# The first MLP matrix: the rounded half of each weight tile by a casting transfer from DRAM instead of a copy on ScalarE

## The chip, the cores and the metric

The kernel runs on one core of a Trainium2 chip. The metric is the device time of one execution in microseconds (us). The kernel before takes 880.09 us, the median of three runs between 879.93 and 880.3 us. The engines are named as in the profile: PE (TensorE, the matrix unit; PEld is its weight load), DVE (VectorE), ACT (ScalarE), POOL (GpSimd) and SP (SyncE, which here only issues transfers). Each engine works through its own list of instructions in order; an instruction that waits holds up what stands behind it on that engine.

## The reference

The kernel computes one decoder layer on 512 tokens of width 1024 in float32: a normalised input goes to a gated linear recurrence and to sliding-window attention, both are merged and projected, then comes an MLP, a gated embedding and a last normalisation. The change touches the MLP alone:

```python
u = rmsnorm(x, norm_mlp_g[i]) @ w_up[i]                      # 512 x 1024 by 1024 x 4096
x = x + jnp.square(jax.nn.relu(u)) @ w_down[i]               # 512 x 4096 by 4096 x 1024
```

## The kernel before

**Two halves of every number.** PE multiplies operands of type fp32r, a float32 rounded to fewer bits. To keep float32 accuracy, each operand is held as two tiles: a rounded high part and the rest. A weight tile `wr` (128 x 1024 float32, 512 KB, loaded by an SP transfer) is split in two steps: ACT copies it with a cast into `wh` (fp32r), then DVE subtracts, `wl = wr - wh`. A product is then three matmuls: high by high, high by low, low by high. `split` (lines 134 to 141) does both steps, `load_w` (line 155) loads and splits a tile.

**Buffers.** `wr`, `wh` and `wl` have four buffers each (`WRB`, `WB`), shared in turn by all the weights of the kernel. The ACT copy of a tile can begin only when PE has finished with the tile that was four places ahead in the same buffer.

**The MLP.** `up_w(f)` (line 992) fetches tile f of the 32 tiles of `w_up`. The work goes in four quarters q. In each, `up` (line 1107) multiplies eight up tiles, 24 matmuls of 512 columns each; ACT takes the result through relu (`rt`) and square (`F`), DVE forms sums of blocks in `F`, and both are split into `uf`. Then `down` (line 1137) uses seven block products in place of eight: 14 weight tiles, 12 matmuls each, formed from eight loaded tiles (`wd`, six buffers, and two `wr` buffers). The results are added by DVE into `xk`, the running sum of the layer (line 1157).

**The entry into the MLP.** `out_proj` (line 997), the projection before the MLP, ends with four block products summed in PSUM tiles X, Y and Z and added by DVE into `xk` (line 1023). The MLP's input `x1` is `xk` transposed on PE (`two_columns_of`, line 983: two of the eight blocks of 128 channels at a time), then split by ACT and DVE (lines 140 and 141). Blocks 0 to 3 are transposed before the last product of `out_proj`, blocks 4 to 7 after its last sum into `xk` rows 256 to 511. `begin_up` (line 1056) interleaves the first two up tiles with this: the first four blocks of tile 0, the transposes of blocks 4 to 7, then the first half of tile 1 and the second halves of both.

**What sets the order.** The program's text gives the dependences; a scheduler that weighs estimated costs lays out each engine's list, so an edit in one place may change the order of other instructions nearby. Transfers issued by SP and by POOL stand in two separate queues, each in order. POOL issues few transfers: around the MLP six that add `q1` into `xk` (line 1033) and, in the last quarter, six that add a scaled product (line 1167).

Of the kernel before, what the change touches and what calls it, by code (L numbers as in the profile page):

```python
# [11 lines left out]
F32R = mybir.dt.float32r  # L12
# [4 lines left out]
P = 128  # L17
# [3 lines left out]
KT = D // P  # L21
# [8 lines left out]
WB = 4  # L30
# [6 lines left out]
def block_kernel(  # L37
# [29 lines left out]
    nc = tc.nc  # L67
    V, A, G, T = nc.vector, nc.scalar, nc.gpsimd, nc.tensor


    def pool(stack, name, **kw):
        return stack.enter_context(tc.tile_pool(name=name, bufs=1, reuse_waits="tile", **kw))
# [4 lines left out]
    wp = pool(ctx, "wp")  # L77
# [9 lines left out]
    def nm(s):  # L87
        n_names[0] += 1
        return f"{s}_{n_names[0]}"
# [30 lines left out]
    def tk(n):  # L120
        return tp_.tile([P, NH * (DV + 1)], F32, tag="tk", bufs=4, name=nm(n))
# [7 lines left out]
    def r32(t):  # L129
        return t.bitcast(F32)  # L130

    last_low = [None]

    def split(dst, src, scale=None):

        if scale is None:
            A.copy(dst[0], src)  # L137
            last_low[0] = V.tensor_sub(dst[1], src, r32(dst[0]))  # L138
        else:
            A.activation(dst[0], src, AF.Copy, scale=scale)  # L140
            V.scalar_tensor_tensor(dst[1], src, scale, r32(dst[0]), ALU.mult, ALU.subtract)
# [8 lines left out]
    def load_raw(src, n):  # L150
        raw = wp.tile([P, 1024], F32, tag="wr", bufs=WRB, name=nm("wr"))
        nc.sync.dma_start(out=raw[:, :n], in_=src)
        return raw

    def load_w(src, n, dims, raw=None):

        if raw is None:
            raw = load_raw(src, n)
        parts = [wp.tile([P, 1024], F32R, tag=t, bufs=WB, name=nm(t))[:, :n] for t in ("wh", "wl")]
        split(parts, raw[:, :n])  # L160
        return [q.rearrange("p (k c) -> p k c", k=dims) for q in parts]
# [178 lines left out]
    for m in range(NT):  # L340
# [10 lines left out]
        t = sp.tile([P, 256], F32, tag="vs", bufs=4, name=nm("vs"))  # L351
# [127 lines left out]
    for m in range(NT):  # L479
        t = tk("vm").rearrange("p (h d) -> p h d", h=NH)  # L480
# [87 lines left out]
    with tc.issue_after(last_mm[0].ins):  # L568
        for t in range(NT):
            for s in range(t + 1):  # L570
                c = (t * NT + s) * 4
                T.transpose(pgc[:, c : c + 4], gg[t][:, s * P : (s + 1) * P], ident[:4, :4])
            c = (NT * NT + t) * 4
# [416 lines left out]
            split(dst[k + c], ps[:, c, :], g[:, k + c : k + c + 1])  # L990

    def up_w(f):
        return load_w(w_up[f], KT * P, KT)

    _, x1 = big_hl("x1")

# [59 lines left out]
    def begin_up():  # L1056

        ps, w = [ps_g(), ps_g()], [up_w(0), up_w(1)]

        def part(f, k):  # L1060
            mm_T(ps[f], [q[:, k : k + 4, :] for q in w[f]], x1[k : k + 4], k == 0, k == 4)

        part(0, 0)
        two_columns_of(x1, 4, gmlp)
        two_columns_of(x1, 6, gmlp)
        part(1, 0)
        part(0, 4)
        part(1, 4)
        return ps
# [37 lines left out]
    def up(q, uf):  # L1107
        fs = None
        for f in range(8):
            if q == 0 and f < 2:  # L1110
                ps = begun[f]
            else:
                ps = ps_g()
                mm_T(ps, up_w(q * 8 + f), x1)
            a = mp.tile([P, 512], F32, tag="rt", bufs=3, name=nm("rt"))
            A.activation(a, ps, AF.Relu)
            if f % 2 == 0:
                fs = F()
            o = 2 * (f % 2)
            done = A.activation(fs[:, o : o + 2, :].rearrange("p a b -> p (a b)"), a, AF.Square)  # L1120
            if q == 0 and f == 2:
                with tc.issue_after(done.ins):
                    squares()
            if f % 2:
                hl = [np_.tile([P, 7 * 256], F32R, tag="uf", bufs=8, name=nm("uf")) for _ in range(2)]

                cut = 3 * 256 if f == 7 else 0
                if cut:
                    split([t[:, :cut] for t in hl], fs[:, 1:4, :].rearrange("p a b -> p (a b)"))
                V.tensor_add(fs[:, S1, :], fs[:, A21, :], fs[:, A22, :])  # L1130
                V.tensor_sub(fs[:, S3, :], fs[:, A11, :], fs[:, A21, :])
                V.tensor_sub(fs[:, S2, :], fs[:, S1, :], fs[:, A11, :])
                V.tensor_sub(fs[:, S4, :], fs[:, A12, :], fs[:, S2, :])  # L1133
                split([t[:, cut:] for t in hl], fs[:, 1 + cut // 256 :, :].rearrange("p a b -> p (a b)"))
                uf.append(hl)
# [302 lines left out]
```

## Time and profile before

| What | Value |
|---|---|
| Time, median of three runs | 880.09 us |
| The profiled execution, its own time | 879.82 us |
| Its span, first to last instruction | 878.0 us |
| PE busy | 866.8 us of the span |
| DVE busy | 657.2 us |
| ACT busy | 483.5 us |
| POOL busy | 34.1 us |
| Granted PE clock, mean | 0.998 |

The profile page gives the busy time of each engine, the span in forty slices, the chain of waits that ended last, and the costliest groups of instructions. A timeline row reads: start, duration, engine, line, operation, output tile `<-` input tiles, shape, count, and in brackets the idle time of that engine before it with what ended it. The landing time of a transfer counts from its issue to its last byte's signal. A line number can be that of a helper: all weight splits stand under lines 137 (ACT) and 138 (DVE).

### The profile page before, as it was taken

Reading aid. Unit: us, or ns where it says so; the run is one execution under the profiler, and the core shown is the slowest. Engines: PE = TensorE matmul, PEld = TensorE weight load, DVE = VectorE, ACT = ScalarE, POOL = GpSimd, SP = SyncE. Lnnn points to the kernel's source line nnn. Section 1 sums busy time; section 2 is a strip of 40 time slices with the busy share of each in tenths; the row PEclk is TensorE's granted clock in tenths of the full one; section 3 lists DMA queues with packets and bytes.
Section 4 is the critical chain, followed back from the end, with each engine's and each line's share of the span. In section 5 each row is a group of like instructions: output and inputs, shape, how many; then the busy total and the mean of one; then the engine's idle time right before and its main releaser. Section 6 shows DMA issues by size and latency. Waiting matters only on the chain.

```text
span 878.0 us, 11545 instructions
## 1 busy us (share of the span) xinstructions
PE 866.8 (99%) x4372; PEld 725.6 (83%) x4372; DVE 657.2 (75%) x966; ACT 483.5 (55%) x803; POOL 34.1 (4%) x58
## 2 busy tenths in 40 slices
PE   8999999999999999999999999999999999999996
PEld 7888889998777777788888888888888888888886
DVE  6999887875789876665896669756956794698557
ACT  6684554544676768743344665356435634564843
POOL 1111010000000000000020000000000000020000
PEclk9999999999999999999999999999999999999999
DMA  7765244435122162274244612530352054125302
GB/s 266 211 180 186 73 150 169 165 111 196 52 73 72 49 199 88 97 240 144 72 75 145 236 49 71 197 106 10 124 185 75 1 186 149 49 52 141 121 0 96
DMA packets 32793, 106.74 MB, mean 122 GB/s; under 512 B 4573, under 2 KB 4573, under 8 KB 32738
## 3 DMA queue, kind: packets, MB, share of 16 engines
q1 hardware_dynamic: 27570, 93.15, 31.2%
q0 software_dynamic: 5024, 12.59, 5.9%
q8 instruction: 34, 0.56, 0.3%
q10 hardware_dynamic: 144, 0.26, 0.1%
q14 instruction: 21, 0.17, 0.1%
HBM read 91.30 MB, written 8.40 MB: 114 GB/s over the span
## 4 chain that ended last, share of the span: by engine, by line
PE 90%; DVE 4%; ACT 3%; DMA 2%; issue 1%; SPq 0%; ACTq 0%; DVEq 0%
PE psg L171 50%; PE psp L171 23%; PE psa L171 7%; PE pst L171 4%; PE psa L831 1%; PE pst L747 1%; DVE wl L138 1%; DMA wr<-in_w_vsif 1%; ACT lm L712 1%; PE psa L819 1%; PE psa L689 1%; PE psa L690 1%; ACT wh L137 0%; DMA wr<-in_w_gb 0%; PE psp L980 0%
## 5 line engine op out<-in xcount | busy, mean ns | idle before, releaser
L137 ACT CAST wh<-wr 128x1024 fp32r<-128x1024 f32 x138 | 144.8, 1051 | 180.3 <-PE psg L171 74.8
L138 DVE TENSOR_TENSOR wl<-wr,wh 128x1024 fp32r<-128x1024 f32 x138 | 167.8, 1219 | 85.9 <-ACT wh L137 84.6
L171 PE MATMUL psg<-x,wh 128*128 128x512 f32 x512 | 157.7, 389 | 0.0
L171 PE MATMUL psp<-wh,uf 128*128 128x512 f32 x448 | 138.6, 389 | 0.0
L171 PEld LDWEIGHTS psg<-x,wh 128*128 128x128 f32 x512 | 96.0, 188 | 19.9
L171 PE MATMUL psg<-x,wl 128*128 128x512 f32 x256 | 99.6, 389 | 0.0
L171 PEld LDWEIGHTS psp<-wh,uf 128*128 128x128 f32 x448 | 84.1, 188 | 17.5
L171 PE MATMUL psp<-wl,uf 128*128 128x512 f32 x224 | 87.2, 389 | 0.0
L171 PE MATMUL psg<-h,wh 128*128 128x512 f32 x256 | 81.1, 395 | 0.7 <-DVE rc L715 0.7
L137 ACT CAST wh<-wd 128x1024 fp32r<-128x1024 f32 x44 | 46.2, 1052 | 54.0 <-PE psp L171 21.9
L138 DVE TENSOR_TENSOR wl<-wd,wh 128x1024 fp32r<-128x1024 f32 x44 | 53.1, 1217 | 14.7 <-ACT wh L137 14.5
L171 PEld LDWEIGHTS psg<-x,wl 128*128 128x128 f32 x256 | 48.0, 188 | 10.0
L171 PEld LDWEIGHTS psg<-h,wh 128*128 128x128 f32 x256 | 47.0, 188 | 11.2 <-issue 1.6
L171 PE MATMUL psg<-h,wl 128*128 128x512 f32 x128 | 50.5, 395 | 0.0
L138 DVE TENSOR_TENSOR uf<-F,uf 128x1792 fp32r<-128x1792 f32 (+2 forms) x20 | 33.0, 1652 | 21.8 <-ACT uf L137 21.8
L171 PEld LDWEIGHTS psp<-wl,uf 128*128 128x128 f32 x224 | 42.0, 188 | 8.7
L171 PE MATMUL psg<-yb,wh 128*128 128x512 f32 x128 | 41.3, 402 | 0.1
L171 PE MATMUL psg<-ya,wh 128*128 128x512 f32 x128 | 39.5, 390 | 0.0
L137 ACT CAST uf<-F 128x1792 fp32r<-128x1792 f32 (+2 forms) x20 | 27.9, 1396 | 20.5 <-DVE F L1133 20.4
L1157 DVE SCALAR_TENSOR_TENSOR xk<-psp,r,xk 128x512 f32<-128x512 f32 x48 | 33.7, 744 | 5.5 <-PE psp L171 5.2
L171 PE MATMUL psg<-hS,wh 128*128 128x256 f32 x192 | 35.6, 284 | 0.0
L171 PE MATMUL psa<-h,wh 128*128 128x256 f32 x192 | 35.3, 285 | 0.2 <-ACT p L625 0.2
(322 smaller groups left out, 1745.6 us busy)
## 6 DMA issues: line engine op xcount, KB each, us to landing
wr<-in_w_up SPq DMA_DIRECT2D x32, 512.0 KB, 3.3
wd<-in_w_down SPq DMA_DIRECT2D x24, 512.0 KB, 3.7
wr<-in_w_qsw SPq DMA_DIRECT2D x8, 512.0 KB, 4.3
gd<-gr POOLq DMA_DIRECT2D x8, 512.0 KB, 3.7
wr<-in_w_qkml SPq DMA_DIRECT2D x8, 512.0 KB, 3.2
wr<-in_w_b SPq DMA_DIRECT2D x8, 512.0 KB, 3.2
gl<-gd SPq DMA_DIRECT2D x8, 512.0 KB, 3.4
wr<-in_w_a SPq DMA_DIRECT2D x8, 512.0 KB, 4.4
```

Of the source, the lines that this page charges most:

```text
L137: A.copy(dst[0], src)
L138: last_low[0] = V.tensor_sub(dst[1], src, r32(dst[0]))
L171: last_mm[0] = T.matmul(ps, l, r, start=first and i == 0, stop=last and i == len(ops) - 1, skip_group_check=parts)
L689: T.matmul(o, q[:, n * P : (n + 1) * P], kk[kp][ab][:, k0 : k0 + 256], start=True, stop=False)
L690: T.matmul(o, q[:, n * P : (n + 1) * P], kl[kp][ab][:, k0 : k0 + 256], start=False, stop=True)
L712: A.activation(lm3[:, g, :], lm3[:, g, :], AF.Exp, bias=nmx[:, g : g + 1], scale=0.125, accum_out=sm[:, g : g + 1])
L747: T.matmul(o[HALF[ab], :], v[:, c : c + 64], w[:, ab * 512 : (ab + 1) * 512], start=j == 0, stop=j == len(terms) - 1)
L819: T.matmul(psc, qk[4 + h][:, n0 : n0 + P], qk[h][:, n0:], start=True, stop=True, skip_group_check=True)
L831: last_mm[0] = T.matmul(pn[:, t % 2, : DV + 1], wT[s][:, t * P : (t + 1) * P], vm[s][:, h, :], start=s == 0, stop=s == t, skip_group_check ...
L1157: V.scalar_tensor_tensor(o, ps[:, t, :], r2[:, 2 * toks + t : 2 * toks + t + 1], o, ALU.mult, ALU.add)
```

## The change

For the 32 tiles of `w_up`, the SP load into `wr` stays and DVE's subtraction stays. ACT's cast into `wh` is left out; in its place POOL issues a transfer that reads the same 512 KB of `w_up` from DRAM a second time and casts it to fp32r on the way into `wh`.

```diff
     def up_w(f):
-        return load_w(w_up[f], KT * P, KT)
+        raw = load_raw(w_up[f], KT * P)
+        parts = [wp.tile([P, 1024], F32R, tag=t, bufs=WB, name=nm(t)) for t in ("wh", "wl")]
+        nc.gpsimd.dma_start(out=parts[0], in_=w_up[f])
+        last_low[0] = V.tensor_sub(parts[1], raw, r32(parts[0]))
+        return [q.rearrange("p (k c) -> p k c", k=KT) for q in parts]
```

The lists of the engines move with it. The first place is DVE at the entry into the MLP. `wl_4660`, `wl_4666`, `wl_4771` and `wl_4826` are the low halves of up tiles 0 to 3, `x_809` is the low half of the MLP's input (blocks 0, 2, 1, 3, then 4, 6, 5, 7), and `xk_3977`, `xk_3978` are rows 256 to 511 of the running sum, whose last addition the transposes of blocks 4 to 7 read. Before:

```order
L138 TENSOR_TENSOR wl_4660<-wr_4657,wh_4659 128x1024
L1023 TENSOR_TENSOR xk_3975<-psp_4369,xk_3975 128x512
L1023 TENSOR_TENSOR xk_3976<-psp_4369,xk_3976 128x512
L138 TENSOR_TENSOR wl_4666<-wr_4663,wh_4665 128x1024
L138 TENSOR_TENSOR wl_4771<-wr_4768,wh_4770 128x1024
L141 SCALAR_TENSOR_TENSOR x_809_4366<-psp_4609,gmlp,x_808_4365 128x512
L141 SCALAR_TENSOR_TENSOR x_809_4366<-psp_4622,gmlp,x_808_4365 128x512
L141 SCALAR_TENSOR_TENSOR x_809_4366<-psp_4609,gmlp,x_808_4365 128x512
L141 SCALAR_TENSOR_TENSOR x_809_4366<-psp_4622,gmlp,x_808_4365 128x512
L1023 TENSOR_TENSOR xk_3977<-psp_4370,xk_3977 128x512
L1023 TENSOR_TENSOR xk_3978<-psp_4370,xk_3978 128x512
L138 TENSOR_TENSOR wl_4826<-wr_4823,wh_4825 128x1024
```

In the changed kernel the same stretch of DVE's list reads:

```order
L1027 TENSOR_TENSOR xk_3975<-psp_4369,xk_3975 128x512
L1027 TENSOR_TENSOR xk_3976<-psp_4369,xk_3976 128x512
L996 TENSOR_TENSOR wl_4660<-wr_4657,wh_4659 128x1024
L996 TENSOR_TENSOR wl_4666<-wr_4663,wh_4665 128x1024
L141 SCALAR_TENSOR_TENSOR x_809_4366<-psp_4609,gmlp,x_808_4365 128x512
L141 SCALAR_TENSOR_TENSOR x_809_4366<-psp_4622,gmlp,x_808_4365 128x512
L141 SCALAR_TENSOR_TENSOR x_809_4366<-psp_4609,gmlp,x_808_4365 128x512
L996 TENSOR_TENSOR wl_4771<-wr_4768,wh_4770 128x1024
L141 SCALAR_TENSOR_TENSOR x_809_4366<-psp_4622,gmlp,x_808_4365 128x512
L1027 TENSOR_TENSOR xk_3977<-psp_4370,xk_3977 128x512
L1027 TENSOR_TENSOR xk_3978<-psp_4370,xk_3978 128x512
L996 TENSOR_TENSOR wl_4826<-wr_4823,wh_4825 128x1024
```

The low half of tile 0 moved behind the pair of sums, and that of tile 2 moved from ahead of the four `x` rows to between the third and the fourth.

The second place is POOL's list, which had nothing between the two groups of additions into `xk`. In the changed kernel it reads there (the first four of the 32 new rows):

```order
L1037 DMA xk_3977<-q_818_4403 128x512
L1037 DMA xk_3978<-q_819_4404 128x512
L995 DMA wh_4659<-in_w_up 128x1024
L995 DMA wh_4665<-in_w_up 128x1024
L995 DMA wh_4770<-in_w_up 128x1024
L995 DMA wh_4825<-in_w_up 128x1024
```

The 32 new transfers stand in the order of the tiles, behind the six additions of `q1` and ahead of the six of the last quarter.

## The prediction

> **What bounds the kernel now.** I read the page's busy shares first, then PE in the MLP by stretches, then the timelines of ACT, DVE and PE at the two kinds of places where an up tile follows other weights.
>
> ```profile
> span 878.0 us, 11545 instructions
> PE 866.8 (99%) x4372; PEld 725.6 (83%) x4372; DVE 657.2 (75%) x966; ACT 483.5 (55%) x803; POOL 34.1 (4%) x58
> L137 ACT CAST wh<-wr 128x1024 fp32r<-128x1024 f32 x138 | 144.8, 1051 | 180.3 <-PE psg L171 74.8
> ```
>
> PE is busy for 99% of the span. The ACT casts, 1.05 us each, mostly wait for PE to give a buffer back: ACT is not what PE waits for. Two quarters of the MLP, PE busy in each stretch:
>
> ```profile
> 566.50:648.10 81.60, 81.60 (x362) 67.57 (x361) 58.38 (x64) 39.07 (x43) 0.00 (x0) 1.00 0.31 104
> 648.10:729.70 81.60, 81.60 (x362) 67.57 (x361) 58.39 (x64) 39.08 (x43) 0.00 (x0) 1.00 0.31 103
> ```
>
> A quarter is 8 x 24 + 14 x 12 = 360 matmuls in 81.60 us, one per 0.2267 us, with no idle time and full clock. The quarters repeat to the hundredth. So nothing that is taken from ACT here can shorten the MLP; what the change can do is make a weight late.
>
> **What it removes.** 32 casts of 1.05 us, 33.6 us of ACT's 483.5 us. Worth nothing: in these stretches ACT is busy for 39 of 81.6 us and PE for all of it, and outside the MLP no instruction changes.
>
> **What it adds.** 32 issues on POOL, 16.8 MB of reads (32 x 524,288 bytes), and in the path of each up tile a transfer where a cast stood. POOL did nothing in these stretches, so its time is free; what counts is L, the time from issue to landing. No row shows a casting transfer. The nearest rows: an SP load of the same tile; a plain POOL transfer of the same size (`gd`); an accumulating POOL transfer of half the size, where the transfer engines also handle every element (`hS`, a pair; then `xk`, six in a row); and the transfer engines' share and GB/s while such accumulations run alone.
>
> ```profile
> wr<-in_w_up SPq DMA_DIRECT2D x32, 512.0 KB, 3.3
> ...
> gd<-gr POOLq DMA_DIRECT2D x8, 512.0 KB, 3.7
> ```
> ```profile
> L147 POOL DMA_DIRECT2D hS<-s x2: 837/844/852, 51.8 to 52.8; - x2
> ...
> DMA to landing us min/median/max: 3.2/3.5/3.7
> ```
> ```profile
> L1033 POOL DMA_DIRECT2D xk<-q x6: 866/1640/2459, 449.2 to 452.0; - x6
> ...
> DMA to landing us min/median/max: 3.3/5.5/8.6
> ```
> ```profile
> 788.00:791.00 3.00, 1.00 1.07 183
> 791.00:794.00 3.00, 1.00 1.11 194
> ```
>
> Lower end: the cast costs nothing and L is 3.3 us. Upper end of what the rows support: it runs at the accumulating rate, so 3.3 us for the first 256 KB and 0.262 MB / 187 GB/s = 1.4 us for the rest, 4.7 us. I take 4.6: an accumulation reads its target too, but it is the only transfer here in which values are worked on.
>
> The Trainium skill ("DMA: Bandwidth & Descriptors", section "Anatomy of one DMA") fits a POOL-issued transfer at 2.0 us plus bytes over 436 GB/s; worked out from that page, an estimate, 512 KB would take 3.2 us, and the first term below would be nothing instead of 1.1 us. This trace has 3.7 us at the median for a plain one of that size.
>
> **Entry into the MLP, first term.** The order moved here. ACT, DVE and PE before:
>
> ```profile
> 473.57 1.05 ACT L137 CAST wh<-wr 128x1024 fp32r<-128x1024 f32 x1 [1.67 <-PE psp L171]
> 476.29 1.06 ACT L137 CAST wh<-wr 128x1024 fp32r<-128x1024 f32 x1 [1.67 <-PE psp L171]
> 479.01 1.05 ACT L137 CAST wh<-wr 128x1024 fp32r<-128x1024 f32 x1 [1.67 <-PE psp L171]
> ...
> 483.56 1.05 ACT L137 CAST wh<-wr 128x1024 fp32r<-128x1024 f32 x1 [0.20 <-PE psp L171]
> ```
> ```profile
> 480.09 1.23 DVE L138 TENSOR_TENSOR wl<-wr,wh 128x1024 fp32r<-128x1024 f32 x1 [1.38 <-ACT wh L137]
> 481.23 2.91 DVE L141 SCALAR_TENSOR_TENSOR x<-psp,gmlp,x 128x512 fp32r<-128x512 f32 x4
> 484.06 1.28 DVE L1023 TENSOR_TENSOR xk<-psp,xk 128x512 f32<-128x512 f32 x2
> 485.26 1.22 DVE L138 TENSOR_TENSOR wl<-wr,wh 128x1024 fp32r<-128x1024 f32 x1
> 487.83 3.13 DVE L141 SCALAR_TENSOR_TENSOR x<-psp,gmlp,x 128x512 fp32r<-128x512 f32 x4 [1.36 <-ACT x L140]
> ```
> ```profile
> 486.04 1.91 PE L988 MATMUL psp<-ident,xk 128*128 128x128 f32 x16
> 487.70 0.71 PE L171 MATMUL psg<-x,wh 128*128 128x512 f32 x2
> ```
>
> The four casts are up tiles 0 to 3; each begins when PE frees its buffer, and so will the transfers. The 16 transposes at 486.04 need the pair of sums at 484.06: it ended at 484.06 + 1.28 = 485.34, 0.7 us early. In the new list that pair stands behind the subtractions of tiles 1 and 2, and DVE cannot pass them. Tile 1 is issued at 476.29 and lands L later; a hand-over from PE to POOL and from transfer to DVE I put at 0.2 us together (POOL leaves 0.16 to 0.20 us between two issues in these rows).
>
> ```profile
> 36.89 0.84 POOL L147 DMA_DIRECT2D hS<-s  x1 [0.16 <-issue]
> 37.93 0.85 POOL L147 DMA_DIRECT2D hS<-s  x1 [0.20 <-issue]
> ```
>
> Then come tile 1's subtraction (1.14 from 480.09 to 481.23), the four x rows (484.06 - 481.23 = 2.83), tile 2's subtraction among them (1.14) and the pair (1.28): 476.29 + L + 0.2 + 1.14 + 2.83 + 1.14 + 1.28 = 482.88 + L. The fourth transpose, the first that reads the second sum of the pair, is due at 486.04 + 3 x 1.66/16 = 486.35. So PE stands for L - 3.47 us: nothing at L = 3.3, 1.2 us at 4.7, and 1.1 us at 4.6. The transfer engines are free then (share 0.01 and 0.58):
>
> ```profile
> 473.00:477.00 4.00, 4.00 (x20) 3.30 (x18) 2.20 (x4) 1.76 (x2) 0.00 (x0) 1.00 0.01 1
> 477.00:483.00 6.00, 6.00 (x36) 5.22 (x35) 4.52 (x6) 3.66 (x6) 0.00 (x0) 1.00 0.58 193
> 483.00:493.00 10.00, 10.00 (x54) 8.51 (x53) 6.39 (x10) 4.11 (x6) 0.00 (x0) 1.00 0.93 348
> ```
>
> **Entry, second term.** Tile 3's buffer comes free at 483.56, and its subtraction stands ahead of the x rows of blocks 4 to 7. Those end at 483.56 + L3 + 0.2 + 1.14 + 3.13 = 488.03 + L3. The matmul that needs the last of them: after 487.70, 12 matmuls of tile 1, then block 7's second one, the 11th: 487.70 + 22 x 0.2267 = 492.7. PE is late by L3 - 4.7 us. This transfer meets the crowd of 483 to 493, six loads of `w_down` and two of `w_up`, whose own landings were
>
> ```profile
> L1103 SPq DMA_DIRECT2D wd<-in_w_down x6: 327/426/447, 483.5 to 488.3; - x6
> ...
> DMA to landing us min/median/max: 4.6/5.5/8.1
> ```
>
> With L3 at the median, 5.5 us, 0.8 us. Both terms count from the same clock, so the later one decides and they do not add: 1.1 us. From below: L3 at 4.6 gives nothing. From above: 5.5 + 1.4 for the accumulating rate gives 2.2 us. SP softens the crowd: raw tile 7, with four `w_down` loads queued behind it, waits for the subtraction of tile 3 to give a buffer back, so those loads now follow that transfer.
>
> **The later quarters.** Up tile 0 of the second quarter:
>
> ```profile
> 558.73 1.05 ACT L137 CAST wh<-wr 128x1024 fp32r<-128x1024 f32 x1 [1.67 <-DMA wd<-in_w_down]
> ...
> 566.69 0.62 PE L171 MATMUL psg<-x,wh 128*128 128x512 f32 x2
> 567.14 0.39 PE L171 MATMUL psg<-x,wl 128*128 128x512 f32 x1
> ```
>
> Its low half is needed at 567.14; 558.73 + L + 0.2 + 1.22 stays below that for L up to 7.0 us. The next tiles come free 2.72 us apart and are needed 24 x 0.2267 = 5.44 us apart, so each has 2.72 us more. I take nothing, covered by that lead; the cover is gone at L = 7. DVE's other work (sums into `F`, the split of `uf`) sits behind the waiting subtractions, but `uf` is not read before the down half.
>
> **Sum.** 879.82 + 1.1 = 880.9 us for the profiled execution, whose span is 878.0; it stood 0.27 us under the median of 880.09, so 881.2 against the median. About 0.2%, 1.8 us, is what a measurement of this kernel can tell from no change.
>
> **Rivals.** *A crowded tile 3.* L3 between 6.4 and 9 us gives 1.8 to 4.3 us, slower. If the engines serve both queues in turn while SP's loads run, a tile at the accumulating rate needs twice its 2.8 us, and 1.9 us around that (3.3 - 1.4): L3 = 7.5, a stall of 2.8 us, 882.6 us. For it: the crowd rows, whose longest landing is 8.1 us; against it: the transfer is alone on its queue and most of SP's loads move behind it. It decides from L3 = 6.4 us. The Trainium skill ("DMA: Bandwidth & Descriptors", section "Queues, rings and completion order") has each engine alternate between queues packet by packet, which would make this case the rule; the crowd rows, all from one queue, cannot show it.
>
> *The cast at half the accumulating rate.* 512 KB then takes 2 x 2.8 us and 1.9 us around it, 7.5 us even uncrowded. The first term becomes 4.0 us; with 1.5 us of loads in its way in the later quarters, L = 9 costs 2.0 us three times. 879.82 + 4 + 6 = 890 us, slower. Against it: nothing in the trace moves so slowly; for it: nothing in the trace casts.
>
> *A gain.* If something freed on ACT shortened the chain at the MLP's end or start. PE has no idle time in the MLP, so over 1.8 us is not to be found there; below 879.82 only by drift.
>
> **Chances.** The forecast, a stall of 0 to 1.8 us at the entry, 0.50: its own range is 879.9 to 881.9. The crowded tile 3 has 0.29 and the slow cast 0.17, both slower: 0.46. A gain has 0.04. The range of 879.9 to 887 takes in the forecast, the first rival and the milder part of the second.
>
> **What would show it.** In the new profile: POOL with 32 issues more and ACT with 32 casts fewer; the landing of `wh<-in_w_up`, 4 to 5 us; a gap on PE before the transposes of `xk` near 486 us of about a microsecond, ended by DVE's sums; quarters of 81.60 us still. I am wrong if PE waits in each quarter for `wl` of its first up tile, if L is over 6 us, or if the spans between quarters grow.

## The result, and the profile after

The changed kernel takes 882.25 us (median of 6 runs, 881.22 to 884.14) beside 880.28 us for the kernel before (6 runs, 879.93 to 880.91): a ratio of 1.0025, 95% interval 1.0014 to 1.0037. Two more sets of runs of the same kernel, below, gave 1.0034 and 1.0028. So the change costs 2.0 us by the medians and 2.2 us by the ratio. That lies inside the range of 879.9 to 887.0 us, 1 us above the forecast of 881.2 and just above the forecast's own range, 879.9 to 881.9. It is slower, by more than the 0.2% that the prediction takes as its bound, though the interval reaches from 0.14% to 0.37% and so does not clear that bound. The runs also lie further apart: 3 us where the kernel before had 1 us.

The profiled execution took 881.68 us, 0.6 us under the median. From its page, the span, the busy times and the groups that changed (busy us, mean ns of one, idle time ahead and what ended it; for transfers the size and the median landing):

```profile
span 879.9 us, 11593 instructions
PE 866.9 (99%) x4372; PEld 725.2 (82%) x4372; DVE 657.7 (75%) x966; ACT 451.3 (51%) x771; POOL 51.1 (6%) x90
L996 DVE TENSOR_TENSOR wl<-wr,wh 128x1024 fp32r<-128x1024 f32 x32 | 39.2, 1223 | 35.3 <-DMA wh<-in_w_up 30.9
wr<-in_w_up SPq DMA_DIRECT2D x32, 512.0 KB, 3.8
wh<-in_w_up POOLq DMA_DIRECT2D x32, 512.0 KB, 4.3
```

POOL issues 32 transfers more, ACT does 32 instructions less, and ACT's 32 us bring nothing: PE's busy time is what it was. DVE's subtractions now wait 30.9 us for the casting transfers. Where that reaches PE is found by measuring the MLP between two rows of ACT that both kernels have, ahead of it and near its end. Before, then after:

```profile
448.11 1.09 ACT L1028 COPY q<-psg 128x512 f32<-128x512 f32 x2
...
774.34 0.59 ACT L1116 ACTIVATE rt<-psg 128x512 f32<-128x512 f32 x1
```
```profile
448.57 1.09 ACT L1032 COPY q<-psg 128x512 f32<-128x512 f32 x2
...
776.20 0.59 ACT L1120 ACTIVATE rt<-psg 128x512 f32<-128x512 f32 x1
```

326.23 us became 327.63. So 1.40 us of the 1.86 us between the two profiled executions was lost here; the other 0.46 us lay ahead of the change's place, where executions of any of these kernels differ by some tenths. Below, "the MLP is late by" is this difference from 326.23 us. In this execution it came from one place, the entry. PE's timeline and that of its weight loads, after:

```profile
486.93 0.50 PE L171 MATMUL psg<-x,wh 128*128 128x512 f32 x1 [0.73 <-DVE x L141]
...
487.49 2.27 PE L988 MATMUL psp<-ident,xk 128*128 128x128 f32 x16
```
```profile
488.12 1.40 PEld L988 LDWEIGHTS psp<-ident,xk 128*128 128x128 f32 x13 [0.38 <-DVE xk L1027]
```

These two are PE's only waits there: behind 490 us, where the second term of the prediction would show, PE runs on without one, and so does the rest of the MLP (500 to 815 us: PE 315.00 of 315). DVE's timeline shows what held `x` and `xk` back:

```profile
480.76 1.23 DVE L996 TENSOR_TENSOR wl<-wr,wh 128x1024 fp32r<-128x1024 f32 x1 [1.54 <-DMA wh<-in_w_up]
481.90 2.25 DVE L141 SCALAR_TENSOR_TENSOR x<-psp,gmlp,x 128x512 fp32r<-128x512 f32 x3
484.98 1.23 DVE L996 TENSOR_TENSOR wl<-wr,wh 128x1024 fp32r<-128x1024 f32 x1 [0.83 <-DMA wh<-in_w_up]
486.12 0.74 DVE L141 SCALAR_TENSOR_TENSOR x<-psp,gmlp,x 128x512 fp32r<-128x512 f32 x1
486.79 1.28 DVE L1027 TENSOR_TENSOR xk<-psp,xk 128x512 f32<-128x512 f32 x2
```

The subtraction of tile 2, at 484.98, waits for its transfer, and the fourth `x` row and the pair of sums stand behind it. The landings of tiles 1 and 2, from POOL's issues at 477.0 and 479.7:

```profile
L995 POOL DMA_DIRECT2D wh<-in_w_up x1: 539/539/539, 477.0 to 477.0; - x1
...
DMA to landing us min/median/max: 3.7/3.7/3.7
```
```profile
L995 POOL DMA_DIRECT2D wh<-in_w_up x1: 531/531/531, 479.7 to 479.7; - x1
...
DMA to landing us min/median/max: 5.2/5.2/5.2
```

Tile 1 had landed by 480.7 us, 1.5 us behind the next SP issue; it took 3.7 us, which is what a plain POOL transfer of this size took before (3.7). Tile 2 met SP's load of raw tile 4, and behind it that of raw tile 5. The load of raw tile 4 was issued at 475.91 before; now it is the first of the two at 479.25, because its buffer comes free only when DVE has subtracted tile 0, and that moved behind a pair of sums. SP's timeline before and after, and the last two numbers of the row of 481 to 484 us (share of the transfer engines, GB/s), before and after:

```profile
475.91 5.76 SPq L152 DMA_DIRECT2D wr<-in_w_up  x3
```
```profile
479.25 3.09 SPq L152 DMA_DIRECT2D wr<-in_w_up  x2
```
```profile
481.00:484.00 3.00, 3.00 (x15) 2.45 (x14) 2.90 (x5) 2.25 (x4) 0.00 (x0) 1.00 0.59 195
```
```profile
481.00:484.00 3.00, 3.00 (x16) 2.47 (x14) 2.90 (x4) 2.04 (x4) 0.00 (x0) 1.00 1.02 384
```

### The profile page after: what moved, and what is told of

It is laid out like the page before. It is cut to its first block, busy times and chain, and to the rows that moved or that the text cites. A ratio compares the mean times of both kernels' runs of the same rounds, so it can differ in the third digit from the quotient of the medians.

```text
span 879.9 us, 11593 instructions
## 1 busy us (share of the span) xinstructions
PE 866.9 (99%) x4372; PEld 725.2 (82%) x4372; DVE 657.7 (75%) x966; ACT 451.3 (51%) x771; POOL 51.1 (6%) x90
## 4 chain that ended last, share of the span: by engine, by line
PE 68%; issue 4%; ACT 3%; DVE 3%; DMA 0%; POOL 0%; POOLq 0%; ACTq 0%
PE psg L171 41%; PE psp L171 20%; PE psa L831 1%; PE pst L747 1%; PE psa L171 1%; ACT lm L712 1%; PE psa L819 1%; PE psa L689 1%; PE psa L690 1%; ACT wh L137 0%; PE psp L980 0%; PE psa L726 0%; DVE wl L138 0%; PE pst L873 0%; DVE qs L425 0%
## 5 line engine op out<-in xcount | busy, mean ns | idle before, releaser
L137 ACT CAST wh<-wr 128x1024 fp32r<-128x1024 f32 x106 | 111.1, 1051 | 121.2 <-PE psg L171 40.9
L996 DVE TENSOR_TENSOR wl<-wr,wh 128x1024 fp32r<-128x1024 f32 x32 | 39.2, 1223 | 35.3 <-DMA wh<-in_w_up 30.9
L1120 ACT ACTIVATE rt<-psg 128x512 f32<-128x512 f32 x32 | 19.0, 592 | 73.1 <-PE psg L171 73.1
```

Of the source, the lines that this page charges most:

```text
L996: last_low[0] = V.tensor_sub(parts[1], raw, r32(parts[0]))
```

## The experiments

**Theory E (entry).** The loss arises at the MLP's entry: DVE stands at a subtraction whose transfer is late, and `x` and `xk`, which PE needs, stand behind it. **Rival Q (quarters).** It arises in the later quarters, where the first up tile of a quarter has the shortest lead. Each experiment is an edit of the changed kernel unless it says otherwise. Differences are to the kernel before in the same set of runs.

| Run | By casting transfer | Median, us (range, runs) | Before | Ratio, 95% interval |
|---|---|---|---|---|
| a1_again | all 32 | 882.3 (881.04 to 885.6, 6) | 880.04 | 1.0034 [1.0021, 1.0047] |
| a2_first4_cast | 4 to 31 | 880.29 (879.91 to 882.83, 11) | 880.04 | 1.0007 [0.9998, 1.0015] |
| a3_only_first4 | 0 to 3 | 881.66 (881.04 to 883.25, 11) | 880.04 | 1.0019 [1.0011, 1.0028] |
| a4_subs_behind | all 32 | 881.6 (880.52 to 882.01, 11) | 880.04 | 1.0016 [1.0007, 1.0024] |
| b3_order_alone | none | 880.04 (879.72 to 880.63, 11) | 880.15 | 0.9997 [0.9988, 1.0006] |
| c1_short_leads_cast | all but 0 to 3, 8, 16, 24 | 880.25 (879.98 to 880.66, 11) | 880.15 | 0.9997 [0.9988, 1.0006] |
| b5_small_raw_4_5 | all 32 | 881.39 (880.72 to 883.26, 11) | 880.15 | 1.0014 [1.0005, 1.0023] |
| d1_leads_cast | all but 8, 16, 24 | 882.18 (880.75 to 884.3, 10) | 880.13 | 1.0021 [1.0012, 1.003] |
| d2_after_beside | all 32 | 883.26 (881.19 to 883.86, 7) | 880.13 | 1.0028 [1.0017, 1.0039] |
| d3_first4_again | 4 to 31 | 880.62 (879.82 to 881.49, 11) | 880.13 | 1.0003 [0.9994, 1.0012] |
| e1_tile3_cast | all but 3 | 881.7 (880.78 to 882.72, 11) | 880.29 | 1.0016 [1.0007, 1.0025] |
| e2_only_tile3 | 3 | 884.19 (883.56 to 886.22, 5) | 880.29 | 1.0049 [1.0035, 1.0062] |

### Entry or quarters

**a1_again**: no edit.

> The changed kernel unedited, to see how its time spreads and whether its stall is at the entry into the MLP each time. Theory E (entry): the whole loss is PE waiting between 484 and 490 us, for the last x row and the last sums into xk, 1 to 2 us, and the spread of the runs is the spread of when the first casting transfers land; about 882.2 us, runs between 881 and 884. Rival Q (quarters): the slower runs lose their time at the first up tile of the later quarters, and the profile shows PE idle there.

+2.3 us. In its profile the entry is late by 1.5 us, by the way used further down, and the MLP by 1.99: PE also waited for `wl` of the first tiles of the second and fourth quarter, whose transfers landed after 6.9 and 7.0 us. Rival Q has a part in this execution.

**a2_first4_cast** keeps ACT's copy for tiles 0 to 3, **a3_only_first4** for all others:

```diff
     def up_w(f):
+        if f < 4:               # a3_only_first4: if f >= 4
+            return load_w(w_up[f], KT * P, KT)
```

> Up tiles 0 to 3 are split as before the change (ACT's cast), the other 28 by the casting transfer. DVE's list at the entry is that of the kernel before. Theory E: no stall, 880.1 to 880.6 us, spread of the runs about 1 us as before. Rival Q: 28 of 32 transfers stay, so at least 1.5 us of the 2 us stay, 881.8 us or more.

> Only up tiles 0 to 3 come by the casting transfer, the other 28 by ACT's cast as before. Theory E: the loss is all there, 881.7 to 883 us. Rival Q: four transfers of 32 cost little, 880.3 to 880.6 us.

Without the first four transfers the time is that of before (+0.25 us, the interval holds 1); with them alone +1.6 us of the 2.3 stay. The 28 later transfers, 7/8 of the change, cost next to nothing at the median. Two of the eleven runs of a2 lay at 882.2 and 882.8, which led to c1 and d3.

**a4_subs_behind** leaves all 32 transfers and makes DVE subtract tile 1 behind the last pair of sums and tiles 2 and 3 behind the `x` rows of blocks 4 to 7 (here and in b3 the lines that note the last sums and `x` rows are left out):

```diff
-        last_low[0] = V.tensor_sub(parts[1], raw, r32(parts[0]))
+        behind = last_sum[0] if f == 1 else last_x[0] if f in (2, 3) else None
+        with tc.issue_after(behind.ins) if behind is not None else ExitStack():
+            last_low[0] = V.tensor_sub(parts[1], raw, r32(parts[0]))
```

> All 32 tiles by the casting transfer, but DVE's subtractions of tiles 1, 2 and 3 stand behind the work that PE waits for: tile 1 behind the last sums into xk, tiles 2 and 3 behind the x rows of blocks 4 to 7. Theory E in its narrow form (the transfer's time does harm only because DVE waits for it ahead of x rows and sums): no stall, 880.1 to 880.7 us. Rival: the weights themselves come too late for PE, or the crowd of loads costs time elsewhere, and 881.5 us or more stay.

In time a miss: 881.6 us is the rival's. The entry is as before, without a wait on PE, though tile 3 landed after 6.3 us; so what did the harm there was DVE's waiting ahead of the `x` rows and sums. Yet the MLP is late by 1.51 us. The waits turned up elsewhere. DVE, then PE's weight loads:

```profile
501.43 1.23 DVE L1000 TENSOR_TENSOR wl<-wr,wh 128x1024 fp32r<-128x1024 f32 x1 [5.53 <-DMA wh<-in_w_up]
```
```profile
513.17 0.30 PEld L171 LDWEIGHTS psg<-x,wh 128*128 128x128 f32 x2 [0.65 <-ACT rt L1124]
```
```profile
569.01 0.19 PEld L171 LDWEIGHTS psg<-x,wl 128*128 128x128 f32 x1 [0.96 <-DVE wl L1000]
```

Tile 4's transfer, landed after 7.3 us, held DVE's sums in `F` back, those `uf`, `uf` ACT, and ACT the PSUM tile that PE needs at 513. The first tile of the second quarter landed after 7.7 us. Taking a late transfer out of one queue's way let others count.

### Order, crowd, or the cast

**b3_order_alone** is the kernel before, with the subtraction of tile 2 moved to where the changed kernel has it:

```diff
+        A.copy(parts[0], raw)
+        behind = xs[1] if f == 2 else None
+        with tc.issue_after(behind.ins) if behind is not None else ExitStack():
+            last_low[0] = V.tensor_sub(parts[1], raw, r32(parts[0]))
```

> Every up tile by ScalarE's copy as before; only DVE's subtraction of tile 2 is moved to where the changed kernel has it, behind the third x row of blocks 0 to 3 instead of ahead of x's rows. No casting transfer is in it. Order alone: tile 2's load is covered by then, as in the kernel before, so the fourth x row is late by one subtraction less its slack, some 0.2 us of TensorE, 880.0 to 880.5 us. Rival, the order is the whole loss and the transfer has no part in it: TensorE waits 1 us or more ahead of its first product of the MLP, 881.5 us or more.

880.04 us, no wait on PE: this move of tile 2 alone costs nothing. (Tile 0's subtraction stayed where it was in this kernel.)

**b5_small_raw_4_5** makes SP's loads of raw tiles 4 and 5 small:

```diff
-        raw = load_raw(w_up[f], KT * P)
+        raw = load_raw(w_up[f][:, :128], 128) if f in (4, 5) else load_raw(w_up[f], KT * P)
+        low = raw[:, :1].broadcast_to([P, 1024]) if f in (4, 5) else raw
 ...
-        last_low[0] = V.tensor_sub(parts[1], raw, r32(parts[0]))
+        last_low[0] = V.tensor_sub(parts[1], low, r32(parts[0]))
```

> All up tiles by the casting transfer, as in the changed kernel, but the plain loads of raw tiles 4 and 5 bring 128 of 1024 columns, 64 KB in place of 512, and the low halves of these two tiles are formed against the first raw column alone, so that part of the computation is left out. If tile 2's casting transfer lands late (5.2 us) because the load of raw tile 4 falls on it: it lands in 3.7 to 4 us, TensorE waits 0.4 us or less in place of 1.3 us at the MLP's entry, 881.0 to 881.3 us. Rival, the load of raw tile 4 has no part in it: tile 2 lands after 5 us or more, and the time stays at 882.2 us.

The landing of tile 2 did what Theory E says:

```profile
L996 POOL DMA_DIRECT2D wh<-in_w_up x1: 531/531/531, 479.6 to 479.6; - x1
...
DMA to landing us min/median/max: 3.9/3.9/3.9
```

DVE no longer waits for it, and PE's wait of 0.73 us ahead of the fourth `x` row is gone. The run makes both loads small and does not tell them apart; in a4, where only that of raw tile 4 falls on tile 2, it landed after 4.5 us. What was left, on PE's weight loads:

```profile
486.96 1.40 PEld L988 LDWEIGHTS psp<-ident,xk 128*128 128x128 f32 x13 [0.31 <-DVE xk L1028]
...
492.35 0.19 PEld L171 LDWEIGHTS psg<-x,wh 128*128 128x128 f32 x1 [0.52 <-DVE x L141]
```

The MLP is late by 0.67 us here, half of the 1.40. The second wait is the prediction's second term: an `x` row behind tile 3, which landed after 4.7 us. The median, +1.24 us, is just over the expected 881.3; the crowd around tile 2 is part of the loss, not all.

### The first tiles of the quarters

**c1_short_leads_cast**, **d1_leads_cast** and **d3_first4_again** (d3 is a2 once more; **d2_after_beside** is the changed kernel beside them):

```diff
     def up_w(f):
+        if f < 4 or f % 8 == 0:     # d1_leads_cast: if f in (8, 16, 24)
+            return load_w(w_up[f], KT * P, KT)
```

> Up tiles 0 to 3 by ScalarE's copy as in a2_first4_cast, and the first tile of each later quarter (8, 16, 24) too; the other 25 by the casting transfer. If the two runs of a2_first4_cast that lay 2 us high came from the first tile of a later quarter landing after its cover of 7 us: 880.0 to 880.3 us, and no run more than 1 us above the kernel before. Rival, those runs come from elsewhere: the median is the same, and single runs still lie 2 us high.

> a2_first4_cast once more, for its spread: tiles 0 to 3 by ScalarE's copy, all others by the transfer. If late first tiles of the later quarters exist in some executions: median 880.2 to 880.5 us, and one to three of the executions 1.5 us or more above the kernel before. Rival, the two high executions of a2_first4_cast were an accident: none above 881 us.

> The changed kernel, but the first tile of each later quarter (8, 16, 24) by ScalarE's copy; tiles 0 to 3 and the other 25 by the casting transfer. If the entry costs about 1.4 us and late first tiles of quarters cost the rest (0.3 to 0.8 us for each that lands 7 us or later): 881.4 to 881.7 us, 0.5 us or more below the changed kernel beside it. Rival, the quarters have no part in it: the time of the changed kernel, 882.2 us.

> The changed kernel unedited, beside d1_leads_cast on the same chip: 882.0 to 882.5 us by both theories.

c1 is the kernel before in time and spread. But d3's highest run lay 1.4 us above before, not the two microseconds of a2's, and before itself reached 1 us above its median in that set: the tail of a2 was not found again, and neither expectation of d3 holds. d1 stands 1.1 us under d2 with overlapping intervals, but it was to lie at 881.4 to 881.7 (882.18 is its rival's number), and d2 at 882.0 to 882.5: both missed, and as a test of rival Q inconclusive. The medians don't show what the quarters cost; the traces do, in single executions. The profiles of d1 and d2 were worth more for another reason: in both the MLP was late by over 3 us, with no wait in the later quarters. d2, tile 3's landing, then PE:

```profile
L995 POOL DMA_DIRECT2D wh<-in_w_up x1: 528/528/528, 484.3 to 484.3; - x1
...
DMA to landing us min/median/max: 7.1/7.1/7.1
```
```profile
486.77 0.50 PE L171 MATMUL psg<-x,wh 128*128 128x512 f32 x1 [0.47 <-DVE x L141]
493.44 0.50 PE L171 MATMUL psg<-x,wh 128*128 128x512 f32 x1 [0.83 <-DVE x L141]
494.94 0.50 PE L171 MATMUL psg<-x,wh 128*128 128x512 f32 x1 [0.29 <-DVE x L141]
```

The waits at 493.44 and 494.94 are for the low `x` rows of blocks 4 and 5. Tile 3's landing orders all profiled executions in which the first four tiles come by transfer and DVE keeps the changed order. The lateness at the entry is read at the MLP's first `rt<-psg` row, which stands 46.74 us behind the `q<-psg` row in the changed kernel and 45.33 us in c1, whose MLP took 326.21 us; for a3, where another instruction of ACT stands in front of that row, it is that of the whole MLP.

| Execution | Tile 2 landed after | Tile 3 landed after | Entry late by | Tile 3's landing less 4.0 |
|---|---|---|---|---|
| b5_small_raw_4_5 | 3.9 | 4.7 | 0.68 | 0.7 |
| the changed kernel | 5.2 | 5.3 | 1.41 | 1.3 |
| a1_again | 5.0 | 5.5 | 1.51 | 1.5 |
| d2_after_beside | 4.9 | 7.1 | 3.08 | 3.1 |
| a3_only_first4 | 5.3 | 7.2 | 3.26 | 3.2 |
| d1_leads_cast | 5.0 | 7.7 | 3.69 | 3.7 |

Tile 2 lands alike in the last five; tile 3 does not, and the last three entries follow it. The agreement of the second row is a coincidence: PE's waits in that execution are both behind tile 2, which costs nearly the same there. In a1 PE waits behind tile 2 and again, at 492.92 us, behind tile 3.

### Tile 3 alone

**e1_tile3_cast** and **e2_only_tile3**:

```diff
     def up_w(f):
+        if f == 3:                  # e2_only_tile3: if f != 3
+            return load_w(w_up[f], KT * P, KT)
```

> The changed kernel, but tile 3 by ScalarE's copy; DVE's order is that of the changed kernel. The traces so far show the MLP late by tile 3's landing less 4.0 us where that lands in 7.1 us or more (three executions), and by tile 2's 5.2 us through the first of the MLP's products where it lands sooner. If so, the first term alone is left: 881.0 to 881.4 us at the median, and executions above 882 us become rare. Rival, tile 3 only marks a busy stretch and the loss is tile 2's: 882.2 us as in the changed kernel, with executions up to 884 us.

> The kernel before, with tile 3 alone by the casting transfer; DVE's order is that of before. If tile 3's landing decides by itself: the time is 880.1 us plus its landing less 4.0 us, where that is 5 to 7.7 us, so 881 to 883.8 us, with no wait ahead of the products of blocks 0 to 3. Rival, the loss needs tiles 0 to 2 as well: 880.0 to 880.5 us.

e2 shows that tile 3's transfer is enough for such a loss, and goes past the 881 to 883.8 us expected: one transfer, in the old order of DVE, costs 3.9 us, more than all 32 together. It lands after 7.0 us. Its crowd is not that of the changed kernel: raw tile 4 is loaded early again here and SP's three first loads of `w_down` (in `x3`) fall on it at once, where in the changed kernel two of them and raw tile 6 do. SP, the landing, and PE:

```profile
484.00 1.29 SPq L1109 DMA_DIRECT2D wd<-in_w_down  x3
```
```profile
L997 POOL DMA_DIRECT2D wh<-in_w_up x1: 557/557/557, 484.3 to 484.3; - x1
...
DMA to landing us min/median/max: 7.0/7.0/7.0
```
```profile
491.02 0.39 PE L171 MATMUL psg<-x,wh 128*128 128x512 f32 x1
493.29 0.50 PE L171 MATMUL psg<-x,wh 128*128 128x512 f32 x1 [1.88 <-DVE x L141]
```

There is no wait ahead of blocks 0 to 3. The MLP is late by 4.10 us, 1.1 more than the landing less 4.0; the section on the hardware has a likely reason.

e1 keeps 1.4 us; 881.0 to 881.4 was expected, so it is a near miss, and its highest run is 882.72, below the tops of the changed kernel (884.14, 885.6 and 883.86). Its profile is late by 1.36 us at the entry, with tile 2 landed after 5.2 us, and by 2.54 in all. The rest is the first tile of the last quarter:

```profile
L997 POOL DMA_DIRECT2D wh<-in_w_up x1: 528/528/528, 723.7 to 723.7; - x1
...
DMA to landing us min/median/max: 7.9/7.9/7.9
```
```profile
732.89 0.50 PE L171 MATMUL psg<-x,wl 128*128 128x512 f32 x1 [0.53 <-DVE wl L998]
```

This tile's transfer took 7.9 us and made 1.18 us (2.54 - 1.36). So both places cost something in some executions, and among the profiled ones tile 3 the most (over 3 us in a3, d1 and d2).

## Why the prediction was right or wrong

**Casts taken away: nothing.** Right. PE's stretches hold no idle time, and b3 and c1, which differ by 25 casts on ACT, take 880.04 and 880.25 us.

**The landing L of a casting transfer: 4.6 us.** Wrong as a property of the transfer. With little or nothing beside it it lands in 3.4 to 3.7 us (tiles 0 and 1 in the profiled executions), and the cast itself shows no price; the accumulating rate was the wrong row to take. The Trainium skill ("DMA: Bandwidth & Descriptors", section "Anatomy of one DMA") gives 3.2 us for this size by its fit, an estimate; these two tiles take 0.2 to 0.5 us more, and transfers beside SP's loads take up to 7.9 us, which the fit does not cover. The median of 4.3 us that the forecast foresaw came about by crowding.

**Entry, first term: 1.1 us by tile 1 at 4.6 us, tile 2 covered.** The place, the mechanism (subtraction, `x` rows and sums in one queue on DVE) and nearly the size were right (1.41 us), the cause not, so the near size is luck. By the term's own formula tile 1 at 3.7 us would have made 0.2 us. Through tile 2 the same sum is 479.01 + L2 + 0.2 + 1.14 + 0.71 (one `x` row) + 1.28 = 482.34 + L2 against 486.35, so L2 less 4.0: 1.2 us at 5.2. The step that failed is that tile 2's transfer finds the engines free: the row it rested on, 0.58 of the engines in 477 to 483, was read from the old order of SP's loads, and the change moved raw tile 4's load onto tile 2. The part on the change named that tile 0's subtraction moves, but not which buffer waits for it.

**Entry, second term: L3 less 4.7 us, with L3 5.5 us.** Both numbers were too kind. L3 was 5.3, 5.5 and 7.1 us in three profiled executions of the changed kernel, 7.2 and 7.7 in the two others with the same entry. And the lateness is L3 less 4.0. The term took the last of the four `x` rows, block 7's, and when PE reads it. But DVE makes the rows in the order 4, 6, 5, 7 and PE reads the blocks in the order 4, 5, 6, 7, so block 5's row, third on DVE and second on PE, is the one that comes late. With the prediction's own numbers it ends at 483.56 + L3 + 0.2 + 1.14 + 2.35 (three of four rows in 3.13) = 487.25 + L3 and is due 16 matmuls behind 487.70, at 491.33: L3 less 4.1. From d2, on DVE and on PE's weight loads:

```profile
492.64 2.91 DVE L141 SCALAR_TENSOR_TENSOR x<-psp,gmlp,x 128x512 fp32r<-128x512 f32 x4
```
```profile
494.94 0.19 PEld L171 LDWEIGHTS psg<-x,wh 128*128 128x128 f32 x1 [0.60 <-DVE x L141]
```

The third of the four rows ends near 494.8 us, and block 5's second matmul begins at 494.94. That the later of both terms decides and they do not add was right: with tile 3 late (7.1 us and more) the lateness is tile 3's, with tile 3 out of it (e1) tile 2's.

**The rival of a crowded tile 3** (0.29; L3 of 6.4 to 9 us, 882 to 884.4 us) is what the median is closest to: a loss of 2.0 to 2.2 us answers to an L3 of 6.0 to 6.2 us. What spoke against it, that most of SP's loads move behind tile 3, did happen, but two of them and raw tile 6 were left. The Trainium skill ("DMA: Bandwidth & Descriptors", section "Queues, rings and completion order") says that an engine alternates between its queues packet by packet. e2 agrees as far as it goes: a transfer alone on POOL's queue, issued 0.3 us behind SP's first load, took 7.0 us in place of 3.6; in what portions the queues took turns, no run shows.

**The later quarters: nothing, cover gone at L = 7.0.** The bound was about right: 6.9 and 7.0 us in a1 cost 0.48 us in all, 7.9 in e1 1.18, so the cover ends at 6.7 us. What failed is that landings stay below it: the first tiles landed after 3.6 to 7.9 us. In the profiled execution of the changed kernel none was late.

**Sum.** 1.1 us against 2.0 to 2.2. The wide range held because it took in the rival; the forecast's own range did not quite reach. Both terms of the entry are a landing less 4.0 us, and both landings were taken too short: tile 2's as covered, tile 3's as 5.5 us. Which of them makes the median is not shown, since no profiled execution lies at it: at 881.68 us the entry was tile 2's, at 883.41 us tile 3's. Open is what makes tile 3 land after 5.3 us in one execution and 7.1 in the next with the same issue times within 0.3 us, and what the highest runs (884.14 and 885.6 us) had, which no profile caught.

## What to carry to other kernels

A transfer that takes the place of an engine's copy is not priced by its own duration but by the instructions that stand behind its first reader: here a subtraction of 1.2 us on DVE passed on to PE all of the transfer's delay beyond its slack, and two transfers of 32, tiles 2 and 3, made most of the loss. Look first at where the new transfers meet the old loads, and recompute when each load's buffer comes free in the new order, since moving one reader moves a load as well. An engine copy takes the same 1.05 us each time; a transfer in a crowd took 4.4 to 7.9 us here, so it needs a lead for the longest of these, not the median.

## What the runs showed of the hardware that was not expected

PE's granted clock halved after a gap of about 2 us. In e2 PE's product at 491.02 us, 0.23 us by the pace of its neighbours, was followed by the next at 493.29 us, so it stood for 2.0 us; the stretches behind it (clock, engine share and GB/s are the last three numbers):

```profile
491.00:494.00 3.00, 1.12 (x4) 0.30 (x2) 2.56 (x4) 0.73 (x2) 0.00 (x0) 0.97 0.17 37
494.00:497.00 3.00, 3.00 (x7) 2.11 (x7) 1.40 (x2) 0.61 (x1) 0.00 (x0) 0.50 0.92 351
```

For some 3 us the clock was 0.50. PE's last wait for `x` there ends at 494.80 us, and the five matmuls from there to 497.10 took 2.3 us in place of 1.1:

```profile
494.80 0.29 PEld L171 LDWEIGHTS psg<-x,wh 128*128 128x128 f32 x1 [0.50 <-DVE x L141]
...
497.10 0.69 PE L171 MATMUL psg<-x,wh 128*128 128x512 f32 x2
```

That is an estimated 1.2 us lost, enough for the 1.1 us by which e2 lies above tile 3's landing less 4.0; no run tests it apart. In d2, whose longest wait was 0.83 us, and in d1 with 1.33 us, the clock stayed at 1.00. The Trainium skill ("TensorE: Matmul & The Clock Gate", section "What's actually happening") lets the clock fall to half after an idle window of about 3.4 us; in this one execution it fell after PE had stood for 2.0 us, so less was enough.
